# Attention results leave PSUM on two engines and are added on GpSimd; loads of keys, values and plain weights are tied to units of attention

## The chip, the cores and the metric

One core of one Trainium2 chip. The engines are named as in the profile: PE (TensorE), ACT (ScalarE), DVE (VectorE), POOL (GpSimd), and SP (SyncE), which only issues DMAs here. PEld is PE's loading of weights. The metric is the device time of one execution in microseconds; the median of three runs before the change is 2777.72 us (2775.32 to 2780.29).

## The reference

One layer of an encoder, 2048 tokens (a grid of 32 rows by 64) of 1024 features, in float32:

```python
h = rms_norm(x, norm_mix)
q_a, k_a, v_a, q_b, k_b, v_b, g_a, g_b = split(h @ w_in)
y_a = windowed_gqa(q_a, k_a, v_a, sink)          # 8 heads of 64, 2 heads of keys, |t - s| <= 128
y_b = neighborhood_attn(q_b, k_b, v_b, rpb)      # 8 heads of 64, 8 x 16 neighbours on the grid
merged = sigmoid(g_a) * (y_a @ w_proj_a) + sigmoid(g_b) * (y_b @ w_proj_b)
x = x + merged @ w_out
x = x + square(relu(rms_norm(x, norm_mlp) @ w_up)) @ w_down
return rms_norm(x, norm_final)
```

## The kernel before

Products are made of split operands: a float32 matrix is kept as a high part (what TensorE's fp32r format holds) and the low rest, and each product is three matmuls (`mm3`, L193 to L196). PE therefore has most of the work.

**Stages.** The input projections (to about 530 us of the span) turn tiles of `h` and of `w_in` into q, k, v and gates, and store them in HBM. Attention A follows (to about 820), attention B (to about 1138), then the merge with `w_proj_a`, `w_proj_b` and `w_out` (to about 1490), the up projection and the down projection.

**Attention A** has 32 units, `attn_a(g, i)`: two groups of keys by 16 blocks of 128 tokens, four heads in each unit. A unit's first half loads q (L683, three buffers), makes four scores (L690, L691), adds bias and takes the maximum on DVE (L692 to L696), takes the exponential on ACT (L699), and scales by the reciprocal sum on POOL (L703). Its second half turns the probabilities on PE (L709), splits them (ACT `ph` L712, DVE `pl` L713), and multiplies with v into the one bank `av` (L714, L715). **Attention B**, `attn_b(h, j, ...)`, has 32 units too: eight heads by four strips of columns. The lines of the same steps are L818 (q), L821 (v), L831 (scores), L836 to L839 (bias and maximum), L842 (exponential), L846 (scaling), L858 (turning), L863 and L864 (`phb`, `plb`), L869 (bank `av`).

**The eviction.** v stands in two halves, high and low, in the columns of one weight tile. So the bank `av` holds 128 rows, of which the lower 64 (from the high v) and the upper 64 (from the low v) have to be added. ACT copies rows 64 to 127 to SBUF (L718, L876), DVE adds rows 0 to 63 from the bank (L719, L877), and `put` notes the store to HBM; the next unit's second half issues it with `flush` from ACT's queue (L173). As `av` has one buffer, the next unit's first product into it waits for the addition.

**Keys and values.** In A, `load_kv(g, m)` (L670 to L675) loads one half of a group's keys (three DMAs: one of 512 KB, two of 256 KB) and values (512 KB). All four calls are written ahead of the units. In B each head's keys are loaded by `load_k` (L804 to L811), and a bias is made on POOL for three of the four strips (L799) from rows `braw` that SP loads into one buffer (L793).

**Fillers.** What is left of the input projections for the second half of the tokens, four tiles of v and sixteen of gates, is written as a generator of 40 pieces (`fill`). One piece is 24 matmuls into bank `mm`. A tile's weights come through `slice_of`: a load of 512 KB into `raw` (L184, three buffers), a cast on ACT and a subtraction on POOL (`split_weights`, L176, L177) into `whl` (two buffers). `paced` ties each piece behind a product of an earlier unit, `lag` units back, with `tc.issue_after`; that orders what stands on that product's engine, PE. 22 pieces go to A, 18 to B. The loads of a piece are on SP and are not tied.

**Order.** The program is planned ahead of the run: a planner with a model of each instruction's time walks through the program, takes what is ready, and prefers what stands earlier in the text. Each engine then runs its instructions in that order. SP's and ACT's queues also issue the DMAs in order, and a DMA that waits for a buffer, or for an earlier DMA with the same semaphore, holds what is behind it. `tc.issue_after(ins)` puts what its block issues on the engine of `ins` behind `ins`; it orders the issue and waits for nothing else. `drive` starts a unit's first half two units ahead of the second half of the one that PE finishes.

**Memory.** Pools are stacked from both ends of SBUF. Attention A's `ka1`, `va1`, `qa`, `sa` and so on stand on the left, `va0`, `ka0`, `biasa0` on the right, in space that the input projections used. In the merge, the gate of `w_proj_b`'s half is loaded into `z` of the pool `wp` (L1167, L1168), which the fillers use too.

Of the kernel before, what the change touches and what calls it, by code (L numbers as in the profile page):

```python
# [22 lines left out]
P = 128  # L23
KC = D // P
NB = 4
BT = 512
# [66 lines left out]
def encoder_layer(ctx, tc, x, norm_mix, w_in, b_gate, sink, rpb, w_pa, w_pb, w_out,  # L93
# [28 lines left out]
    def T(pl, shape, dt, tag, bufs):  # L122
        n_t[0] += 1
        pl = pl[tag] if isinstance(pl, dict) else pl
        return pl.tile(shape, dt, tag=tag, bufs=bufs, name=f"{tag}_{n_t[0]}")
# [49 lines left out]
    def split_weights(raw, hl):  # L175
        A.copy(hl[:, 0], raw)  # L176
        G.tensor_tensor(out=hl[:, 1], in0=raw, in1=hl[:, 0].bitcast(F32), op=ALU.subtract)  # L177

    def slice_of(parts):

        raw = T(wp, [P, KC, P], F32, "raw", 3)
        at = 0
        for ap, n in parts:
            SY.dma_start(raw[:, at : at + n, :], ap.rearrange("(k p) f -> p k f", p=P))  # L184
            at += n
        hl = T(wp, [P, 2, KC, P], F32R, "whl", 2)
        split_weights(raw, hl)
        return hl
# [438 lines left out]
    masks = pool("masks", side="right", stack=s_m)  # L627
    hpl = pool("hT", side="left", stack=s_h)
    s_a = ExitStack()
    ap_ = pools(s_a, "left", ("ka1", "va1", "qa", "sa", "ph", "pl", "ya", "sta", "biasa1"), "a")  # L630
    ap_.update(pools(s_a, "right", ("va0", "ka0", "biasa0"), "a"))
    b12 = tuple(T(hpl, PAGE, F32R, "hT", 2) for _ in range(2))
    for n, (h, l) in enumerate(zip(*map(halves, b12))):
# [7 lines left out]
    def v_tile(col):  # L641
        hl = slice_of([(cols(w_in[0], col), KC)])
        yield
        for b in (2, 3):
            ps = psum("mm", 2)
            feature_tile(ps, hl, hp[b])
            vt = T(wp, [P, BT], F32, "z", 3)
            A.copy(vt, ps)
            out = v_parts(col, b, vt, psum("mm", 2), T(wp, [P, 1024], F32, "v2", 1))
            for dst, t in out:  # L650
                SY.dma_start(dst, t)
            yield
# [4 lines left out]
    def make_bias_a(g):  # L657
        t = T(ap_, [P, 4, 384], F32, f"biasa{g}", 1)
        dist = t[:, 3]
        SY.dma_start(dist, dist_a)  # L660
        for h in range(4):
            G.tensor_scalar(t[:, h], dist, 2.0 ** -(4 * g + h + 1), 1.0, ALU.mult, ALU.mult)
        bias_a[g] = t

    done, began = [], []

    kas = [T(ap_, [P, 2, S], F32R, f"ka{g}", 1) for g in range(2)]
    vas = [T(ap_, [P, 16, P], F32R, f"va{g}", 1) for g in range(2)]
# [1 line left out]
    def load_kv(g, m):  # L670
        k, kd = kas[g][:, :, m * (S // 2) : (m + 1) * (S // 2)], ks_a[m][g]
        SY.dma_start(k[:, 0].bitcast(F32), kd)
        SY.dma_start(k[0:64, 1].bitcast(F32), kd[64:128])
        SY.dma_start(k[64:128, 1].bitcast(F32), kd[0:64])
        SY.dma_start(vas[g][:, 8 * m : 8 * m + 8].bitcast(F32), vs_a[m][g])  # L675

    def attn_a(g, i):
        c0, c1 = (1 if i == 0 else 0), (2 if i == 15 else 3)
        lo, hi = c0 * P, c1 * P
        n = hi - lo  # L680
        base = (i - 1) * P
        q = T(ap_, [P, 4, P], F32R, "qa", 3)
        began.append(SY.dma_start(q.bitcast(F32), qs_a[g][i // 8][:, i % 8]).ins)  # L683
        ka, v = kas[g], vas[g]
        s = T(ap_, [P, 4, 384], F32, "sa", 4)
        st = T(ap_, [P, 5, 4], F32, "sta", 6)
        mx, nm, sm, es, ri = (st[:, k, :] for k in range(5))
        for h in range(4):
            ps = psum("s", 3)
            PE.matmul(ps[:, :n], q[:, h, :], ka[:, 0, base + lo : base + hi], start=True, stop=False)  # L690
            PE.matmul(ps[:, :n], q[:, h, :], ka[:, 1, base + lo : base + hi], start=False, stop=True)  # L691
            V.tensor_tensor_reduce(out=s[:, h, lo:hi], in0=ps[:, :n], in1=bias_a[g][:, h, lo:hi], scale=1.0,  # L692
                                   scalar=sink_t[:, 4 * g + h : 4 * g + h + 1], op0=ALU.add, op1=ALU.max,
                                   accum_out=mx[:, h : h + 1])
        V.tensor_scalar(nm, mx, -1.0, None, ALU.mult)
        V.tensor_tensor(out=es, in0=sink_t[:, 4 * g : 4 * g + 4], in1=nm, op=ALU.add)  # L696
        A.activation(es, es, AF.Exp)
        for h in range(4):
            A.activation(s[:, h, lo:hi], s[:, h, lo:hi], AF.Exp, bias=nm[:, h : h + 1], accum_out=sm[:, h : h + 1])  # L699
        V.tensor_tensor(out=sm, in0=sm, in1=es, op=ALU.add)  # L700
        V.reciprocal(ri, sm)
        for h in range(4):
            G.tensor_scalar(s[:, h, lo:hi], s[:, h, lo:hi], ri[:, h : h + 1], 1.0, ALU.mult, ALU.mult)  # L703
        yield
        po = psum("av", 1)
        for c in range(c0, c1):
            pt = psum("pt", 2)
            for h in range(4):
                PE.transpose(pt[:, h * P : (h + 1) * P], s[:, h, c * P : (c + 1) * P], ident)  # L709
            ph = T(ap_, [P, 512], F32R, "ph", 3)  # L710
            pl = T(ap_, [P, 512], F32R, "pl", 3)
            A.copy(ph, pt)  # L712
            V.tensor_tensor(out=pl, in0=pt, in1=ph.bitcast(F32), op=ALU.subtract)  # L713
            PE.matmul(po, v[:, i - 1 + c, :], ph, start=c == c0, stop=False)  # L714
            last = PE.matmul(po, v[:, i - 1 + c, :], pl, start=False, stop=c == c1 - 1).ins  # L715
        done.append(last)
        t = T(ap_, [64, 512], F32, "ya", 2)
        A.copy(t, po[64:128, :])  # L718
        V.tensor_tensor(out=t, in0=po[0:64, :], in1=t, op=ALU.add)  # L719
        flush()  # L720
        put(y_a[g].rearrange("(h d) t -> d h t", d=64)[:, :, i * P : (i + 1) * P],
            t.rearrange("d (h q) -> d h q", h=4))
# [18 lines left out]
        while last and live:  # L741
            next(live.pop(0), None)

    def paced(filler, pieces, total, lag):

        for n in range(pieces):
            at = min(n * 32 // total - lag, 31)
            with tc.issue_after(done[at]) if at >= 0 else nullcontext():
                next(filler, None)

    def gate_tile(f, blocks):
        hl = slice_of([(cols(w_in[0], O_GA + f * P), KC)])
        yield
        for b in blocks:
            ps = psum("mm", 2)
            feature_tile(ps, hl, hp[b])
            z = T(wp, [P, BT], F32, "z", 3)
            A.copy(z, ps)
            A.dma_start(zg[b][0][f // 8, (f % 8) * P : (f % 8 + 1) * P, :], z)
            yield  # L760
# [1 line left out]

    fill = chain([v_tile(O_VB + t * P) for t in range(4)] + [gate_tile(f, (2, 3)) for f in range(16)])
    live = []
    for g in range(2):
        make_bias_a(g)
        for m in range(2):
            load_kv(g, m)
    drive((attn_a(g, i) for g in range(2) for i in range(16)), live, True)
    paced(fill, 22, 22, 3)  # L770
    del done[:]
    flush()
    s_a.close()
# [1 line left out]

    s_b = ExitStack()
    bp = pools(s_b, "right", ("braw", "biass", "biasl", "kb0", "qb", "kb1"), "b")
    bp.update(pools(s_b, "left", ("vb", "sb", "phb", "plb", "yb", "stb"), "b"))
    boff, bstart, btotal = bias_layout()
    masks = masks.tile([P, btotal], F32, tag="masks", bufs=1, name="masks_t")  # L780
    with tc.issue_after(began[20]):
# [31 lines left out]
    def attn_b(h, j, k, bias):  # L813
# [1 line left out]
        w, jt = B_W[j], JT[j]  # L815
        kp = 4 * w
        q = T(bp, [P, 4, P], F32R, "qb", 3)
        SY.dma_start(q.bitcast(F32), qs_b[t][e, :, j])  # L818
        yield
        v = T(bp, [P, 8, P], F32R, "vb", 3)  # L820
        SY.dma_start(v[: 4 * w].rearrange("p (b c) d -> p b (c d)", b=4).bitcast(F32),  # L821
# [49 lines left out]
                              skip_group_check=True).ins  # L871
                    first = False
        done.append(last)

        y = T(bp, [64, BT], F32, "yb", 2)
        A.copy(y, po[64:128, :])  # L876
        V.tensor_tensor(out=y, in0=po[0:64, :], in1=y, op=ALU.add)  # L877
        put(y_b[t].rearrange("(e d) (i j t) -> e d i j t", e=2, i=4, j=4)[e, :, :, j, :],
            y.rearrange("d (i t) -> d i t", i=4))

# [44 lines left out]

    first_y = load_y(0)
    first_load = last_dma[0]
    paced(fill, 18, 14, 4)
    s_h.close()


# [224 lines left out]
    for b in range(NB):  # L1156
# [3 lines left out]
        for f in range(8):  # L1160
            hl = slice_of([(cols(w_pa[0], f * P), 4), (cols(w_pb[0], f * P), 4)])
            parts = []
            for n in range(2):
                ps = psum("mm" if n == 0 else "s", 2 if n == 0 else 3)
                for c in range(4):
                    mm3(ps, hl[:, 0, 4 * n + c, :], hl[:, 1, 4 * n + c, :], yh[n][:, c], yl[n][:, c], c == 0, c == 3)
                g = T(wp, [P, BT], F32, "z", 3) if n else T(p4, [P, BT], F32, "z", 4)  # L1167
                SY.dma_start(g, zg[b][0][n, f * P : (f + 1) * P, :])  # L1168
                A.activation(g, g, AF.Sigmoid, bias=bg[:, 8 * n + f : 8 * n + f + 1])
                V.tensor_tensor(out=g, in0=ps, in1=g, op=ALU.mult)  # L1170
                parts.append(g)
            G.tensor_tensor(out=parts[0], in0=parts[0], in1=parts[1], op=ALU.add)
            A.copy(mh[:, f], parts[0])
            V.tensor_tensor(out=ml[:, f], in0=parts[0], in1=mh[:, f].bitcast(F32), op=ALU.subtract)
            if b == 0:
                with tc.issue_after(first_load):
                    load_wo(f)
# [243 lines left out]
```

## Time and profile before

| | us |
|---|---|
| median of three runs | 2777.72 |
| profiled execution, its own time | 2775.78 |
| its span, first to last instruction | 2773.9 |
| PE busy | 2657.5 (96%) |
| DVE busy | 1648.4 (59%) |
| ACT busy | 1274.8 (46%) |
| POOL busy | 836.1 (30%) |
| mean granted clock of PE | 0.983 |

A time in the span counts from its first instruction. In a window of the trace, "20.00, 13.64 (x61)" says that PE was busy 13.64 of 20 us with 61 instructions; the other engines follow, then the clock that the throttle granted to PE as a share of full speed, the share of time in which the DMA engines were busy, and what they moved. A line of the waits names the instruction that waited, what released it, the sum, how often, and the longest. A line of a timeline has the start, the duration, the engine and line, and the tiles (out<-in); what stands in brackets is the engine's idle time before it and what ended it. PEld, matmul ends and spans on POOL are modelled or rough.

### The profile page before, as it was taken

To read this page: it belongs to the slowest core of one execution; us is meant where nothing else is said; L and a number is where in the kernel's file an instruction comes from. 1 tells how busy PE (TensorE), PEld (TensorE's weight loads), DVE (VectorE), ACT (ScalarE), POOL (GpSimd) and SP (SyncE) were. 2 spreads that over 40 slices of the span, in tenths; PEclk is the share of its full clock that TensorE was granted. 3 is DMA by queue.
4 is the path that set the end of the run, shared out by engine and by line. 5 is a ranking of instruction groups with operands and counts; after the bars stand their busy time and mean duration, and the time that the engine had idled before them with its cause. 6 is when DMAs were issued, how large, how long until landed. Compare 5 with 4: busy or idle time off the path is not lost.

```text
span 2773.9 us, 35174 instructions
## 1 busy us (share of the span) xinstructions
PE 2657.5 (96%) x12248; PEld 2181.0 (79%) x12248; DVE 1648.4 (59%) x2443; ACT 1274.8 (46%) x2252; POOL 836.1 (30%) x669
## 2 busy tenths in 40 slices
PE   7999999899998888999999999989999999999998
PEld 6887778688877777778877788878888788888887
DVE  8655675476655656544335666686554644545666
ACT  6334343376654656534333544454444332332444
POOL 1111231143535554334231355565555000000000
PEclk9999999999998999999999999999999999999999
DMA  5756855845347774756444656564433954445555
GB/s 152 196 150 201 275 200 130 254 112 156 106 130 180 190 190 140 240 157 216 126 160 163 228 171 216 182 207 161 156 137 142 343 190 157 143 152 179 168 191 173
DMA packets 326130, 493.66 MB, mean 178 GB/s; under 512 B 28456, under 2 KB 149544, under 8 KB 323776
## 3 DMA queue, kind: packets, MB, share of 16 engines
q1 hardware_dynamic: 297024, 457.85, 52.6%
q10 hardware_dynamic: 28928, 33.56, 3.8%
q8 instruction: 97, 1.59, 0.2%
q14 instruction: 81, 0.66, 0.1%
HBM read 331.86 MB, written 159.45 MB: 177 GB/s over the span
## 4 chain that ended last, share of the span: by engine, by line
PE 80%; DVE 7%; DMA 6%; ACT 4%; issue 2%; POOL 1%; SPq 0%; ACTq 0%; DVEq 0%; POOLq 0%
PE b L240 14%; PE b L242 14%; PE b L241 14%; PE zb L240 5%; PE zb L242 5%; PE zb L241 5%; PE mm L194 3%; PE mm L195 3%; PE mm L196 3%; PE av L869 2%; PE pt L194 2%; PE pt L196 2%; PE pt L195 2%; PE pt L858 1%; DMA z<-zg 1%
## 5 line engine op out<-in xcount | busy, mean ns | idle before, releaser
L241 PE MATMUL b<-dwh,dah 128*128 128x512 f32 x896 | 348.5, 389 | 0.0
L242 PE MATMUL b<-dwh,dah 128*128 128x512 f32 x896 | 347.7, 389 | 0.0
L240 PE MATMUL b<-dwh,dah 128*128 128x512 f32 x896 | 338.1, 389 | 2.2 <-ACT dwh L236 2.2
L233 POOL TENSOR_TENSOR uc<-uc,uc 128x512 f32<-128x512 f32 x120 | 233.4, 1960 | 209.5 <-issue 135.9
L236 ACT CAST dah<-da 128x1024 fp32r<-128x1024 f32 (+1 forms) x128 | 121.0, 945 | 366.6 <-PE b L242 242.3
L240 PE MATMUL zb<-zh,zwhl 128*128 128x512 f32 x672 | 267.6, 401 | 8.7 <-DVE zc L233 3.8
L237 DVE TENSOR_TENSOR dah<-da,dah 128x1024 fp32r<-128x1024 f32 (+1 forms) x128 | 139.3, 1090 | 223.4 <-ACT dah L236 220.4
L241 PE MATMUL zb<-zh,zwhl 128*128 128x512 f32 x672 | 267.7, 399 | 1.8 <-DVE zh L237 1.8
L242 PE MATMUL zb<-zh,zwhl 128*128 128x512 f32 x672 | 264.3, 399 | 4.6 <-DVE zwhl L237 4.5
L240 PE MATMUL b<-ubh,uwhlb 128*128 128x512 f32 x592 | 230.8, 390 | 2.9 <-ACT mh L1207 1.6
L242 PE MATMUL b<-ubh,uwhlb 128*128 128x512 f32 x592 | 229.6, 389 | 2.6 <-DVE uwhlb L237 2.6
L241 PE MATMUL b<-ubh,uwhlb 128*128 128x512 f32 x592 | 230.4, 389 | 0.0
L233 DVE TENSOR_TENSOR uc<-b,uc 128x512 f32<-128x512 f32 x160 | 108.9, 688 | 189.1 <-PE b L242 152.2
L1311 POOL TENSOR_TENSOR st<-st,power 128x1 f32<-128x1 f32 x16 | 13.5, 857 | 614.3 <-DVE st L1310 614.2
L240 PEld LDWEIGHTS b<-dwh,dah 128*128 128x128 f32 x896 | 168.1, 188 | 37.4 <-ACT dwh L236 2.6
L241 PEld LDWEIGHTS b<-dwh,dah 128*128 128x128 f32 x896 | 168.2, 188 | 34.9
L242 PEld LDWEIGHTS b<-dwh,dah 128*128 128x128 f32 x896 | 168.2, 188 | 34.9
L177 POOL TENSOR_TENSOR whl<-raw,whl 128x1024 fp32r<-128x1024 f32 x52 | 129.1, 2483 | 117.1 <-ACT whl L176 117.1
L240 PEld LDWEIGHTS zb<-zh,zwhl 128*128 128x128 f32 x672 | 127.5, 190 | 42.2 <-issue 4.6
L242 PEld LDWEIGHTS zb<-zh,zwhl 128*128 128x128 f32 x672 | 127.6, 190 | 35.5 <-DVE zwhl L237 5.9
L241 PEld LDWEIGHTS zb<-zh,zwhl 128*128 128x128 f32 x672 | 128.0, 191 | 31.2 <-DVE zh L237 2.1
L237 POOL TENSOR_TENSOR zwhl<-zraw,zwhl 128x1024 fp32r<-128x1024 f32 (+1 forms) x24 | 57.5, 2401 | 255.6 <-ACT zwhl L236 254.0
(248 smaller groups left out, 6451.2 us busy)
## 6 DMA issues: line engine op xcount, KB each, us to landing
at<-uc SPq DMA_DIRECT2D x224, 256.0 KB
da<-at SPq DMA_DIRECT2D x96, 512.0 KB
dw<-in_w_down_dram SPq DMA_DIRECT2D x160, 256.0 KB
uraw<-in_w_up_dram SPq DMA_DIRECT2D x32, 1024.0 KB
zraw<-in_w_in_dram SPq DMA_DIRECT2D x22, 1024.0 KB
z<-zg SPq DMA_DIRECT2D x64, 256.0 KB
raw<-in_w_in_dram SPq DMA_DIRECT2D x20, 512.0 KB
xin<-in_x_dram SPq DMA_DIRECT2D x16, 512.0 KB
```

The lines of the kernel that those rows point to most:

```text
L177: G.tensor_tensor(out=hl[:, 1], in0=raw, in1=hl[:, 0].bitcast(F32), op=ALU.subtract)
L194: PE.matmul(ps, lh, rh, start=first, stop=False)
L195: PE.matmul(ps, lh, rl, start=False, stop=False)
L196: PE.matmul(ps, ll, rh, start=False, stop=last)
L233: return eng.tensor_tensor(out=out, in0=a, in1=b, op=op).ins
L236: A.copy(hi, src)
L237: eng.tensor_tensor(out=lo, in0=src, in1=hi.bitcast(F32), op=ALU.subtract)
L240: PE.matmul(ps, lh, rh, start=first, stop=False, skip_group_check=True)
L241: PE.matmul(ps, lh, rl, start=False, stop=False, skip_group_check=True)
L242: PE.matmul(ps, ll, rh, start=False, stop=last, skip_group_check=True)
L858: PE.transpose(pt[:kp, at + (i - i0) * P : at + (i - i0 + 1) * P], s[i][:, rr : rr + kp], ident)
L869: last = PE.matmul(po[:, i0 * P : (i0 + ni) * P], v[:kp, c, :], src[:kp, o : o + ni * P], start=first, stop=(c == 7 and z == 1), skip_grou ...
```

## The change

Three parts. (1) A new helper `both_parts` takes the place of the eviction in both attentions: ACT copies the upper half, DVE copies the lower half into a tile of its own (`ya0`, `yb0`, one buffer each), and POOL adds the two in SBUF. (2) In A only the first bias and the first `load_kv` are written ahead of the units. The other loads, and the second bias, are written before units 4, 8 and 12 and queued behind the q loads of units 2, 6 and 10. (3) The loads of `slice_of` are queued behind the q load of a unit that `paced` works out; in B the q loads are noted for it in `began_b`. And `z` in `wp` has two buffers in place of three.

```diff
+    load_after = [None]
+
     def slice_of(parts):
         raw = T(wp, [P, KC, P], F32, "raw", 3)
         at = 0
         for ap, n in parts:
-            SY.dma_start(raw[:, at : at + n, :], ap.rearrange("(k p) f -> p k f", p=P))
+            with tc.issue_after(load_after[0]) if load_after[0] else nullcontext():
+                SY.dma_start(raw[:, at : at + n, :], ap.rearrange("(k p) f -> p k f", p=P))
             at += n
...
+    def both_parts(pl, tag, po):
+
+        t, lower = T(pl, [64, 512], F32, tag, 2), T(pl, [64, 512], F32, tag + "0", 1)
+        A.copy(t, po[64:128, :])
+        V.tensor_copy(lower, po[0:64, :])
+        G.tensor_tensor(out=t, in0=t, in1=lower, op=ALU.add)
+        return t
...
-        t = T(ap_, [64, 512], F32, "ya", 2)
-        A.copy(t, po[64:128, :])
-        V.tensor_tensor(out=t, in0=po[0:64, :], in1=t, op=ALU.add)
+        t = both_parts(ap_, "ya", po)
         flush()
...
-    def paced(filler, pieces, total, lag):
+    def paced(filler, pieces, total, lag, loads):
         for n in range(pieces):
             at = min(n * 32 // total - lag, 31)
+
+            soon = (n + 2) * 32 // total - lag + 2
+            load_after[0] = loads[min(soon, 31)] if soon >= 0 else None
             with tc.issue_after(done[at]) if at >= 0 else nullcontext():
                 next(filler, None)
+        load_after[0] = None
...
-    for g in range(2):
-        make_bias_a(g)
-        for m in range(2):
-            load_kv(g, m)
-    drive((attn_a(g, i) for g in range(2) for i in range(16)), live, True)
-    paced(fill, 22, 22, 3)
+    make_bias_a(0)
+    load_kv(0, 0)
+
+    def all_a():
+        for g in range(2):
+            for i in range(16):
+                n = 16 * g + i
+                if n in (4, 8, 12):
+                    with tc.issue_after(began[n - 2]):
+                        if n == 8:
+                            make_bias_a(1)
+                        load_kv(*{4: (0, 1), 8: (1, 0), 12: (1, 1)}[n])
+                yield attn_a(g, i)
+
+    drive(all_a(), live, True)
+    paced(fill, 22, 22, 3, began)
...
-        SY.dma_start(q.bitcast(F32), qs_b[t][e, :, j])
+        began_b.append(SY.dma_start(q.bitcast(F32), qs_b[t][e, :, j]).ins)
...
-        y = T(bp, [64, BT], F32, "yb", 2)
-        A.copy(y, po[64:128, :])
-        V.tensor_tensor(out=y, in0=po[0:64, :], in1=y, op=ALU.add)
+        y = both_parts(bp, "yb", po)
...
-    paced(fill, 18, 14, 4)
+    paced(fill, 18, 14, 4, began_b)
...
-                g = T(wp, [P, BT], F32, "z", 3) if n else T(p4, [P, BT], F32, "z", 4)
+                g = T(wp, [P, BT], F32, "z", 2) if n else T(p4, [P, BT], F32, "z", 4)
```

The two other uses of `z` in `wp`, in `v_tile` and `gate_tile`, get two buffers in the same way, and the pools `ya0` and `yb0` join the lists of pools on the left.

More of the change, by code (lines that the diff above doesn't have):

```diff
@@ L629, in encoder_layer @@
     s_a = ExitStack()
-    ap_ = pools(s_a, "left", ("ka1", "va1", "qa", "sa", "ph", "pl", "ya", "sta", "biasa1"), "a")
+    ap_ = pools(s_a, "left", ("ka1", "va1", "qa", "sa", "ph", "pl", "ya", "ya0", "sta", "biasa1"), "a")
     ap_.update(pools(s_a, "right", ("va0", "ka0", "biasa0"), "a"))
@@ L646, in v_tile @@
             feature_tile(ps, hl, hp[b])
-            vt = T(wp, [P, BT], F32, "z", 3)
+            vt = T(wp, [P, BT], F32, "z", 2)
             A.copy(vt, ps)
@@ L663, in make_bias_a @@
         bias_a[g] = t
-    done, began = [], []
+    done, began, began_b = [], [], []
     kas = [T(ap_, [P, 2, S], F32R, f"ka{g}", 1) for g in range(2)]
@@ L756, in gate_tile @@
             feature_tile(ps, hl, hp[b])
-            z = T(wp, [P, BT], F32, "z", 3)
+            z = T(wp, [P, BT], F32, "z", 2)
             A.copy(z, ps)
@@ L777, in encoder_layer @@
     bp = pools(s_b, "right", ("braw", "biass", "biasl", "kb0", "qb", "kb1"), "b")
-    bp.update(pools(s_b, "left", ("vb", "sb", "phb", "plb", "yb", "stb"), "b"))
+    bp.update(pools(s_b, "left", ("vb", "sb", "phb", "plb", "yb", "yb0", "stb"), "b"))
     boff, bstart, btotal = bias_layout()
```

## The prediction

> **What bounds the kernel now.** I read the busy slices of the page first, then stretches of 20 us (windows), the waits of TensorE in the poor ones, and the timelines of the queues behind those waits. In the page's slices PE is the only engine near its limit:
>
> ```profile
> PE   7999999899998888999999999989999999999998
> ```
>
> So only time in which PE idles, or runs at a lower clock, can be won. Attention A runs from 537 to 820 us of the span, B from 820 to 1138. In the windows (span, busy time of PE, PEld, DVE, ACT, POOL, then granted clock, DMA share, GB/s):
>
> ```profile
> 540.00:560.00 20.00, 17.62 (x75) 14.87 (x76) 12.55 (x37) 8.75 (x25) 5.12 (x7) 0.80 0.74 227
> 600.00:620.00 20.00, 20.00 (x109) 17.05 (x108) 12.29 (x34) 11.74 (x28) 7.96 (x11) 1.00 0.39 110
> ...
> 820.00:840.00 20.00, 13.64 (x61) 10.08 (x61) 12.16 (x43) 10.88 (x32) 12.22 (x17) 0.78 0.93 256
> ...
> 860.00:880.00 20.00, 12.85 (x73) 11.27 (x72) 14.07 (x21) 9.19 (x22) 16.11 (x19) 0.80 0.66 175
> ```
>
> Between 560 and 820 PE idles 5.0 us in all (20.00 less busy, summed over 13 windows): that part of A has nothing to give. B idles 47 us, and its clock drops with the idling. The entry to A is the third place. PE's waits there (us, times, longest), and SP's timeline:
>
> ```profile
> PE s L690 <- DMA ks_b<-ze: 7.2, 1, 7.2
> PE s L691 <- DMA ka<-ks_a: 3.7, 1, 3.7
> ```
> ```profile
> 513.14 0.53 SPq L672 DMA_DIRECT2D ka<-ks_a  x1
> ...
> 521.77 0.39 SPq L675 DMA_DIRECT2D va<-vs_a  x1
> ...
> 532.21 0.38 SPq L672 DMA_DIRECT2D ka<-ks_a  x1
> ...
> 536.81 0.74 SPq L674 DMA_DIRECT2D ka<-ks_a  x1
> ```
>
> PE stops at 530.4 after its last filler and gets the first score of group 0 through at 542.4. The keys that end the wait come from the load of 536.81, which the chain of waits follows for 5.51 us to 542.32. The eight loads of 513 to 522 are 3 MB that nobody needs yet: group 1's, whose home is free sooner, and queue and lanes serve them first. In B (PE's own waits, 820 to 1140):
>
> ```profile
> PE av L869 <- DVE yb L877: 20.8, 15, 2.1
> PE pt L858 <- DVE plb L864: 9.8, 7, 5.5
> PE av L869 <- ACT phb L863: 9.0, 3, 4.5
> ```
>
> **The change, part by part.**
>
> *Eviction of the attention bank.* Now: ACT copies the upper half (0.58 us, L876), then DVE adds the lower (0.68, L877), then PE may write the one av bank. After: ACT's copy and a DVE copy side by side, so DVE's 0.68 and a hop of 0.06 leave the chain. One turn on the chain, then ACT's and DVE's timelines:
>
> ```profile
> 941.48 0.59 ACT yb L876
> 942.09 0.69 DVE yb L877
> 942.83 1.53 PE av L869 x9
> ```
> ```profile
> 942.08 1.07 ACT L863 CAST phb<-pt 96x512 fp32r<-96x512 f32 x2
> ```
> ```profile
> 942.70 1.28 DVE L864 TENSOR_TENSOR plb<-pt,phb 96x512 fp32r<-96x512 f32 x2
> ```
>
> PE could start at 942.12. But only the first pair's four matmuls (0.5 us) are then ready. The second pair wants its phb, which ACT casts after the copy (942.08 to 942.66), and the plb after that, at 943.38. That matmul ran at 943.52 before and can run at 943.44. So the turn wins 0.1 us, not 0.74: what is late next is ACT's own queue, exps, copy, cast. 15 such turns: 1.5 us. Bounds: 0 to 15 x 0.74 = 11. In A the same wait is 1.9 us over six turns (PE's waits on DVE ya); I take 1. The new DVE copy is not in the trace: DVE reads of 288 and 512 columns of a bank take 0.45 and 0.69 us (L836), so it costs DVE what the add did.
>
> *The add on GpSimd.* 64 adds on 64x512. The nearest row is L1172, 128x512, 1.30 us: 42 us of POOL in A and in B, where it is busy some 40% and 50%. Its reader is ACT's y store (flush), no longer DVE's next instruction. Two costs follow. First, DVE's small operations stop while POOL adds. DVE's timeline and then POOL's:
>
> ```profile
> 868.13 6.19 DVE L839 TENSOR_SCALAR stb<-stb 128x4 f32<-128x4 f32 x1
> ```
> ```profile
> 868.21 2.34 POOL L177 TENSOR_TENSOR whl<-raw,whl 128x1024 fp32r<-128x1024 f32 x1
> 870.51 3.77 POOL L799 TENSOR_TENSOR biasl<-braw,masks_t 128x384 f32<-128x384 f32 x3
> ```
>
> L839 has four columns, takes 0.16 us at best, and ended when POOL's additions did; PE then idled 5.54 us. The Trainium skill (GPSIMD Engine Reference, Specifications) says why: GpSimd's SBUF interfaces are shared with VectorE and contend with DVE's 2-port modes and with its two-input operations. The trace agrees (6.19 us), and the rule speaks against this change. How often would it strike? The add can start when POOL's four scalings (L846, 2.1 to 2.5 us from the reciprocal on) are done and then ends 3 to 4 us after the bank's copy. Laid into the trace, it ends 0.1 to 0.6 us before the next L839 in six turns of B (954.19 against 954.35), runs into it by 0.1 to 0.6 in three, and is far from it in most others. I take 1 us lost, bounds 0 and 13 (the third rival).
>
> Second, the store waits in ACT's queue for POOL, and casts stand behind it. I take 1 us, bounds 0 and 30 (second rival).
>
> *Loads of keys and v in A.* Eight of sixteen, then four, leave the entry. What remains there: bias, group 0's first 1.5 MB, three q, ks_b's stores. Group 0's home is free when the last zb matmul has read zwhl (524.7). At best the key loads go out at once, and the third lands 1.2 us of issue and 5.5 of transfer later: 531.5. At worst SP still puts four ks_b stores between the first and the second, as at 532.68 to 536, and nothing moves: 542.4. I take 533.5, a little over the best since the queue is emptier than the one that the 5.51 us was measured in, yet stores remain: 8.9 us, bounds 0 and 10.9. Clock: after the stop the filler's matmuls stood 0.43 apart, not 0.23, nine of them, 1.7 us; I leave that as a bonus that a shorter stop may not bring. The moved loads (12, 4.5 MB) now come beside units 2 to 12, where DMA is busy 0.39; q has three buffers, 24 us of lead, against some 7 us for 1.5 MB.
>
> *Loads of plain weights.* Each raw load goes behind a q load, about three units (24 us) ahead of its matmul, where it used to go three slices ahead, when a buffer came free. SP stood 57 us in A and 36 around B at L184 for that buffer; PE felt little of it, as the waits above show. At the entry 1.5 MB of five early slices go too (counted above). What is lost is lead: ACT's cast whl could now wait for its load (3.8 to 12.7 us from issue to landing in A) with casts of ph behind it. I take 1 us, bounds 0 and 8 (eleven slices by a cast's 0.7).
>
> *z from three buffers to two.* In the merge, ACT waits for z 44 times, 84 us, and PE hardly (10 us of waits in all from 1140 to 1560). A round trip of one buffer (load some 3, sigmoid 0.72, product 0.69, add 1.29) is about 6 us, two buffers serve an f every 3, and PE needs 5.6 per f. I take 0.5, bounds 0 and 4. In fillers, pieces are 12 to 20 us apart: nothing.
>
> Sum: -8.9 - 1.5 - 1 + 1 + 1 + 1 + 0.5 = -7.9 us. The profiled execution took 2775.78 (span 2773.9 and 1.9 around it), so 2767.9; it lies 1.9 under the median of 2777.72, and on that basis the forecast is **2769.8, say 2769**.
>
> **Rivals.**
>
> 1. *The bank was what held B.* If the new order also brings phb earlier, the 15 turns win 0.74 each (11 us). The clock then falls less: rows at 0.78 to 0.96 over B's 318 us are a loss of about 27 us (one less the clock, times the window, summed), of which I give a third, 9. With the entry's 9: 2777.7 - 29 = 2749. For: 20.8 is the largest wait in B. Against: the turn above. 0.14.
>
> 2. *The store blocks ACT (slower).* POOL works in order and waited for braw at L799 11 times, 52.8 us, up to 13.0. An add placed behind such a wait holds the y store, it holds ACT, and phb is late. The trace has one such stop, from another cause: the store of 1008.89 waited from 1003.4 (5.5 us), and PE lost 4.46. Laid behind POOL's bursts, the adds of 861, 893, 930 and 993 would end 9 to 17 us after the store's present place, 48 us together, of which PE would feel 0.8. With half of them so placed: 24 x 0.8 = 19 us, 3 more for the clock, less 9 for the entry: 2791. It decides from two of the four on; with one it is even. 0.19.
>
> 3. *The shared interface.* If every add of B meets an L839, it is late by up to 1.3 us. Delays of 2.19, 1.53 and 1.31 us cost PE 1.25, 0.65 and 0.38 in the trace: about 0.4 for 1.3, 32 times, 13 us; less 8, 2783. This is the rule cited above from the Trainium skill; three meetings in 32 speak against so much. 0.07.
>
> 4. *The entry stays.* SP's order is planned anew, and stores or a late first weight slice (the filler of 524.7 to 530 needs it) may take the place of group 1's keys. Then -0.0 to +2: 2778. 0.16.
>
> Forecast: 0.44.
>
> **How the numbers follow.** A measurement tells about 0.2% (5.6 us) from no change: faster is below 2772.2, slower above 2783.3. The forecast's own range is 2761 to 2774, nine tenths of it faster. Faster: 0.40 + 0.14 + 0.02 = 0.56. Slower: 0.19 + 0.03 (of rival 3) = 0.22. Same: 0.22. Range for eight in ten: 2747 to 2788; that leaves out about half of rival 1 and half of rival 2.
>
> **What would show it.** Right: the first A score before 535 and no half-clock row at 540; A's other windows at 19.5 or more; B's wait of av on the bank gone, but one on phb or plb in its place of nearly the same size. Wrong: an ACT store L173 that waits for POOL several us (rival 2), L839 with many durations over 1 us (3), PE waiting for ka beyond 540 (4), or B's windows above 19 at clock 1.00 (1). What I can't see is the planned order after the change: every number of B rests on ACT keeping exps, copy, cast.

## The result and the profile after

The changed kernel takes 2820.26 us in the median (2817.23 to 2829.38); the kernel before, run beside it, 2776.52. The ratio is 1.0163, 95% interval 1.0135 to 1.0191: 44 us slower, where 2769 was forecast. The profiled execution took 2822.0 us, with a span of 2820.2 (before 2773.9) and a mean clock of 0.975 (0.983).

The first question is in which stage the time went. From PE's timeline, in us of the span ("A" from the first score to the last product of attention A, "B" from there to the last product of attention B):

| | first score | A | B | rest | span |
|---|---|---|---|---|---|
| before | 537.7 | 282.3 | 316.4 | 1637.5 | 2773.9 |
| after | 538.6 | 288.6 | 362.1 | 1630.9 | 2820.2 |
| difference | +0.9 | +6.3 | +45.7 | -6.6 | +46.3 |

Nearly all of it is attention B. Two things make it up. PE idles 71.1 us in B, for 47.1 before. And the same 1546 matmuls keep it busy 291.0 us, for 269.3, at a mean granted clock of 0.854, for 0.914. The lower clock is enough for that: 269.3 x 0.914 / 0.854 is 288. So of the 45.7 us, 24 are idle time and 22 are matmuls that take longer. (The rest has the same 7087 matmuls, and PE idles 25.2 us in it, for 29.9; e16 comes back to this.) The page's busy slices of the changed kernel, and the granted clock under them, show the same place:

```profile
PE   7999999899998877899999999999999999999998
PEclk9999999999998888899999999999999999999999
```

The windows, with the columns of the prediction:

```profile
540.00:560.00 20.00, 19.66 (x93) 16.32 (x92) 8.89 (x33) 6.99 (x23) 1.84 (x4) 0.91 0.63 174
...
700.00:720.00 20.00, 16.80 (x85) 13.15 (x83) 15.30 (x25) 11.72 (x29) 18.53 (x21) 1.00 0.33 91
820.00:840.00 20.00, 14.79 (x62) 10.01 (x61) 12.41 (x37) 11.23 (x31) 9.49 (x12) 0.91 0.48 141
860.00:880.00 20.00, 14.14 (x64) 12.45 (x65) 8.73 (x22) 10.64 (x26) 13.12 (x14) 0.66 0.47 130
```

The row of 540 is better than it was (19.66 for 17.62): PE no longer stops a second time behind the first score, but that score is no earlier. At 860 the clock falls to 0.66. What PE, and then ACT, waited for in B (820 to 1190; us, times, longest):

```profile
PE av L892 <- DVE yb L684: 41.5, 17, 7.1
PE av L892 <- ACT phb L886: 17.7, 8, 7.1
```
```profile
ACT phb L886 <- POOL yb L685: 19.4, 3, 8.4
ACT whl L176 <- DMA raw<-in_w_in_dram: 17.5, 4, 7.3
...
ACT yb L683 <- POOL yb L685: 10.8, 1, 10.8
...
ACT z L771 <- POOL yb L685: 6.7, 1, 6.7
```

The wait of `av` on the bank did not go, it doubled (20.8 before), and ACT has two waits that it did not have in the kernel before: 36.9 us for POOL's addition (19.4 + 10.8 + 6.7), and 17.5 for `raw`. One stop in full, from the timeline of all engines:

```profile
859.87 2.96 POOL L822 TENSOR_TENSOR biass<-braw,masks_t 128x288 f32<-128x288 f32 x3 [7.57 <-DMA braw<-tab]
862.80 1.25 POOL L685 TENSOR_TENSOR yb<-yb,yb 64x512 f32<-64x512 f32 x1
...
864.08 0.55 ACTq L173 DMA_DIRECT2D y_b<-yb  x1
864.73 0.48 ACT L886 CAST phb<-pt 128x384 fp32r<-128x384 f32 x1 [8.44 <-POOL yb L685]
...
865.26 0.58 PE L892 MATMUL av<-phb,vb 128*128 128x256 f32 x1 [7.12 <-ACT phb L886]
```

Read it downwards: POOL waits 7.57 us for `braw`, makes the bias, and only then the addition that stands behind it. The store in ACT's queue waits for the addition, the cast behind the store idles 8.44 us, and PE 7.12. That is the mechanism of the prediction's second rival. The eviction itself, from another window of the same timeline:

```profile
920.02 0.58 ACT L683 COPY yb<-av 64x512 f32<-64x512 f32 x1
...
920.71 0.68 DVE L684 COPY yb<-av 64x512 f32<-64x512 f32 x1 [0.50 <-ACT yb L683]
```

The two copies are not side by side. DVE's begins 0.11 us after ACT's end, in the median of the 64 units 0.10, and what it waits for is ACT. The bank leaves after 1.37 us in the median, for 1.30 with the addition before: no sooner.

### The profile page after: what moved, and what is told of

It reads as the page before. It is cut to its first block, busy times and chain, and to the rows that moved or that the text cites. A ratio compares the mean times of both kernels' runs of the same rounds, so it can differ in the third digit from the quotient of the medians.

```text
span 2820.2 us, 35092 instructions
## 1 busy us (share of the span) xinstructions
PE 2677.6 (95%) x12248; PEld 2199.3 (78%) x12248; DVE 1644.7 (58%) x2443; ACT 1275.6 (45%) x2252; POOL 916.7 (33%) x733
## 4 chain that ended last, share of the span: by engine, by line
PE 67%; DMA 5%; DVE 3%; ACT 2%; POOL 2%; issue 1%; SPq 0%; ACTq 0%; POOLq 0%; DVEq 0%
PE b L243 14%; PE b L244 14%; PE b L245 14%; PE mm L197 3%; PE mm L198 3%; PE mm L199 3%; PE pt L197 2%; PE pt L198 2%; PE pt L199 2%; DMA braw<-tab 2%; PE av L892 2%; PE pt L720 1%; ACT sb L865 1%; PE pt L881 1%; PE s L197 1%
## 5 line engine op out<-in xcount | busy, mean ns | idle before, releaser
L243 PEld LDWEIGHTS b<-dwh,dah 128*128 128x128 f32 x896 | 168.1, 188 | 36.9 <-ACT dwh L239 2.0
L244 PEld LDWEIGHTS zb<-zh,zwhl 128*128 128x128 f32 x672 | 126.8, 189 | 31.7 <-DVE zh L240 3.1
```

The lines of the kernel that those rows point to most:

```text
L243: PE.matmul(ps, lh, rh, start=first, stop=False, skip_group_check=True)
L244: PE.matmul(ps, lh, rl, start=False, stop=False, skip_group_check=True)
```

## The experiments

The theories at the start. **Store**: the y store waits in ACT's queue for POOL's addition, and casts wait behind it. **Late**: ACT's cast of a tied weight slice waits for its load, and casts of `phb` wait behind it. Rivals: POOL's 42 us of additions in each attention are themselves too much; the two z buffers; the bank. Ratios are to the kernel before, run beside each kernel, with 95% intervals; they are not quotients of the medians.

### The parts one at a time

e1: the changed kernel with the old eviction.

```diff
-        t = both_parts(ap_, "ya", po)
+        t = T(ap_, [64, 512], F32, "ya", 2)
+        A.copy(t, po[64:128, :])
+        V.tensor_tensor(out=t, in0=po[0:64, :], in1=t, op=ALU.add)
```
and the same in B.

> The changed kernel with the old eviction (ACT copies the upper half, DVE adds the lower from the bank); the tied loads, the later keys and the two z buffers stay. Theory E (the eviction: the store waits in ACT's queue for POOL's addition): most of the loss goes, 2775 to 2785 us; what is left is the late raw load, up to 10 us. Theory L (the tied weight loads hold ACT's casts): the loss stays, 2805 to 2820. In the trace of the changed kernel ACT waited 42 us for POOL's additions and 17.5 us for raw in attention B; shared out by these, the loss of 44 us would be 31 of E and 13 of L, so about 2789.

Measured: 2803.58 us, ratio 1.0095 (1.0079 to 1.0111): below theory L's range, and 15 us above the shared figure.

e2: the kernel before with `both_parts` (the diff above the other way round) and two z buffers.

> The kernel before with the new eviction alone, and two z buffers in place of three, without which the new tiles have no room. Loads as before. Theory E: 2805 to 2820 us, with POOL's additions again ending the waits of ACT's phb casts in attention B. Theory L: 2775 to 2785. Shared out by ACT's waits: about 2808.

Measured: 2800.98 us, 1.0090 (1.0072 to 1.0109): below theory E's range.

e3: the kernel before with `load_after`, `began_b` and the new `paced`, and nothing else of the change.

> The kernel before with one part of the change alone, the weight loads of slice_of queued behind units' q loads. Theory E: within 8 us of before, 2777 to 2785, ACT's whl cast waiting a little for raw. Theory L: 2800 or more, with ACT's whl cast waiting 15 us or more for raw in attention B. Shared out by ACT's waits: about 2789.

Measured: 2808.26 us, 1.0107 (1.0087 to 1.0126).

e4: the kernel before with `all_a` in place of the four early calls of `load_kv`.

> The kernel before with one part alone, the keys and values of attention A after the first half group loaded behind the units 2, 6 and 10. By the prediction's step the first score comes 8.9 us earlier and the time is about 2768. By the rival that the entry stays, 2776 to 2779: the trace of the changed kernel has the first score at 538.6 (537.7 before), so I expect this one.

Measured: 2776.07 us, 0.9986 (0.9971 to 1.0001); first score at 540.1.

By stage (B against before): e1 +29.1, e2 +26.1, e3 +32.2 us. So there are two losses of nearly one size, 23 us (e2) and 30 (e3) alone, and 44 together. Sharing the loss out by ACT's waits (31 to 13) was wrong: the tied loads alone cost more than twice what that gave. The keys and values cost nothing and bring nothing that can be told; the first score comes no earlier. What e3's ACT waited for in B (820 to 1140), and one stop:

```profile
ACT whl L176 <- DMA raw<-in_w_in_dram: 43.0, 6, 11.0
```
```profile
898.49 0.43 SPq L187 DMA_DIRECT2D raw<-in_w_in_dram  x1
...
905.98 1.04 ACT L176 CAST whl<-raw 128x1024 fp32r<-128x1024 f32 x1 [11.05 <-DMA raw<-in_w_in_dram]
...
909.66 0.56 DVE L871 TENSOR_TENSOR plb<-pt,phb 128x384 fp32r<-128x384 f32 x1 [0.18 <-ACT phb L870]
...
910.37 0.45 PE L865 MATMUL pt<-ident,sb 128*128 128x128 f32 x1 [6.97 <-DVE plb L871]
```

ACT came to the cast at 894.9, before SP had even issued the load; the load took 7.5 us, the cast came 0.03 us after it landed, and the exponentials and the cast of `phb` stood behind it. Of the eight casts from 780 to 1130 us seven waited, 46.9 us in all. In the kernel before none did. For comparison, the load and the cast of the same slice in e5, where the tie is four units earlier:

```profile
844.55 0.43 SPq L187 DMA_DIRECT2D raw<-in_w_in_dram  x1
...
864.71 1.05 ACT L176 CAST whl<-raw 128x1024 fp32r<-128x1024 f32 x1
```

There the load takes 10.7 us, longer than in e3, but has landed 9 us before the cast, which waits for nothing.

### The price of the store, of POOL and of the buffers

e5 is told with the ties below. e6: e2 with all stores that `flush` issues on SP's queue, those behind attention B included.

```diff
     def flush(keep=0):
         while len(pending) > keep:
-            A.dma_start(*pending.pop(0))
+            SY.dma_start(*pending.pop(0))
```


> The kernel with the new eviction alone (e2_evict_only, 2801 us), but the y stores are issued from SP's queue in place of ACT's. Theory 'store' (the y store waits in ACT's queue for POOL's addition, and casts, exponentials and fillers' copies wait behind it): ACT no longer waits for POOL's yb, most of the 23 us goes, 2778 to 2787. Rival 'POOL' (the 42 us of additions on POOL delay the bias and the scaling, or stop DVE): stays at 2795 or more.

Measured: 2785.52 us, 1.0033 (1.0016 to 1.0050).

e7: e2 with the addition on DVE.

```diff
-        G.tensor_tensor(out=t, in0=t, in1=lower, op=ALU.add)
+        V.tensor_tensor(out=t, in0=t, in1=lower, op=ALU.add)
```


> The kernel with the new eviction alone (e2_evict_only, 2801 us), but DVE adds the two halves in SBUF in place of POOL. The bank still leaves by ACT's copy and then DVE's, the store stays in ACT's queue. Theory 'store' and rival 'POOL' both say that the loss goes: 2778 to 2790, a few us above before since DVE has 0.7 us more in each unit. If it stays at 2800, it is neither: then it is the copy by DVE, the order of the copies or the two z buffers.

Measured: 2781.28 us, 1.0019 (1.0003 to 1.0035).

e15: the kernel before with two z buffers and a spare addition.

```diff
         V.tensor_tensor(out=y, in0=po[0:64, :], in1=y, op=ALU.add)
+        spare = T(bp, [64, 512], F32, "yb0", 1)
+        G.tensor_tensor(out=spare, in0=y, in1=y, op=ALU.add)
```


> The kernel before with the old eviction, two z buffers, and behind each eviction a spare addition of the same size on POOL, whose result nobody reads. Theory 'store': POOL's additions themselves cost little, 2776 to 2785 us. Rival 'POOL' (its queue is late for scaling and bias, or it stops DVE's small operations): 2795 or more.

Measured: 2778.91 us, 1.0024 (1.0004 to 1.0045). There are 64 additions, in A too, as many as in the change. But they read one tile twice, and take 1.03 us each, where the change's take 1.28 (medians): 66 us of POOL for 82.

e16: the kernel before with `"z", 2` for `"z", 3` in all three places.

> The kernel before with two z buffers in place of three and nothing else. The prediction took 0.5 us for it, bounds 0 and 4: 2776 to 2780. If it is the 5 us that stay in e7_add_dve: 2781 to 2783.

Measured: 2767.43 us in the median, below both expectations, ratio 0.9990 (0.9974 to 1.0007): no difference that can be told. But the traces show one. Behind attention B, PE idles 25.0 to 27.5 us in all ten kernels with two z buffers, and 28.9 to 31.7 in all ten with three, and nearly all of the difference lies 350 to 900 us behind B's end. That accounts for most of the 6.6 us by which the rest of the changed kernel is shorter; why a smaller pool does this stays open.

ACT's waits for POOL's addition in B, in e2:

```profile
ACT sb L848 <- POOL yb L682: 11.5, 2, 5.9
ACT phb L869 <- POOL yb L682: 11.1, 2, 7.9
...
ACT z L764 <- POOL yb L682: 8.7, 2, 5.7
...
ACT yb L680 <- POOL yb L682: 6.2, 1, 6.2
```

That is 37.5 us in e2; in e6 and e7 ACT has no such wait, and B is 319.3 and 320.3 us long, for 342.5 in e2 and 316.4 before. So the store in ACT's queue is 22 to 23 us of B. With the additions on POOL and nobody waiting (e15) B is 317.4. e6, e7 and e15 land where theory "store" put them; rival "POOL" at its price (2795 or more) falls. At a smaller price it stays: e16 is e15 without the additions, and 11 us faster (2767.43 for 2778.91; in ratios, 0.9990 for 1.0024). So the additions cost something by themselves, though nobody waits for their results, 9 to 11 us, and about as much as e6 keeps (9 us). e7, which has no addition on POOL but one more operation on DVE, keeps 5. What stays lies in A more than in B: A is 289.1 us long in e6, 286.7 in e7 and 285.3 in e15, for 282.3 before.

### The bank, and both mended

e10: the changed kernel, the weight loads four units earlier.

```diff
-            soon = (n + 2) * 32 // total - lag + 2
+            soon = (n + 2) * 32 // total - lag - 2
```


> The changed kernel with one constant altered: the weight loads are tied four units earlier (as in e5_raw_early). If the parts add, the changed kernel's 2820 falls by the 44 us between e3 and e5, to 2776 to 2782; what stays above e5's 2764 is then the eviction, less than the 23 us it cost alone. If the two losses hid each other's waits (in sum they were 51 and together 44), 2783 to 2790. If the eviction's waits for POOL were themselves caused by late casts, 2770 or less.

Measured: 2800.36 us, 1.0088 (1.0061 to 1.0114): a miss, 10 us above the highest figure. The late loads took 20 us of the changed kernel, not 44.

e11: e10 with e6's edit.

> The changed kernel with the weight loads tied four units earlier and the y stores issued by SP in place of ACT. By theory 'store' the rest of the eviction's price goes but for the 9 us that e6_store_sp kept: 2768 to 2776. If it is no faster than e10_after_raw_early, the store in ACT's queue is not what the eviction costs here.

Measured: 2781.93 us, 1.0015 (0.9999 to 1.0031): 6 us above the expected range, and no longer clearly above the kernel before. The two mendings take 38 of the 44 us: 20 (2820.26 to 2800.36) and 18 (to 2781.93). B is 319.0 us, 2.6 above before.

e12: e10 with the copies in the other order.

```diff
-        A.copy(t, po[64:128, :])
         V.tensor_copy(lower, po[0:64, :])
+        A.copy(t, po[64:128, :])
```


> As e10_after_raw_early, but in the eviction DVE's copy of the lower half is written ahead of ACT's of the upper. In the trace of the changed kernel DVE's copy begins about 0.1 us after the end of ACT's every time. Theory 'one after the other' (the second reader of the bank is ordered behind the first): now ACT's copy begins 0.1 us after DVE's ends, the bank leaves no sooner, and the time is within 8 us of e10, rather above, since ACT's queue now stands for DVE's 0.68 us. If the two copies overlap in this order, the bank leaves 0.6 us sooner and PE's wait of av on the bank halves.

Measured: 2810.53 us, 1.0129 (1.0098 to 1.0160), 10 us above e10, 2 more than expected. In all 64 units ACT's copy now starts after the end of DVE's, at best 0.03 us and in the median 1.53 us behind it; PE waits for ACT's copy:

```profile
PE av L892 <- ACT yb L684: 11.4, 9, 3.5
```

In e10 the same wait of B was 18.5 us (on DVE's copy), so it fell by more than a third, which an overlap would have done too; but the copies overlap in no unit. So whichever copy is written first, the other waits for it: the program orders the two readers of the bank. That the chip would run them side by side is what the Trainium skill gives to expect ("PSUM — Partial Sum Buffer", section "PSUM bank collisions raise a hardware error"): two engines may use one bank at the same time in different groups of 32 partitions, and these are rows 0 to 63 and 64 to 127. No run here shows an overlap, because the order was made ahead of the run; what a true overlap would bring was not tried.

### The ties' lead

e5: e3 with the edit of e10. e13, e17, e18 and e14: the same with `+ 1`, nothing, `- 3` and `- 5` in place of `- 2`, that is one, two, five and seven units earlier than in e3. A unit of B is about 10 us.

> The kernel before with the tied weight loads alone (as e3_raw_only, 2808 us), but tied four units earlier. In e3_raw_only nearly every cast of raw in attention B started within 0.03 us of its load's landing; the loads took 6 to 11.5 us there and were issued at the last moment. Theory 'late' (the tie asks for the load a transfer's time too late, ACT waits in order, casts of phb behind it): no cast waits any more, 2775 to 2783 us. Rival 'tied at all' (the tie rearranges the planned order, or the loads collide with those of B): stays above 2795.

> As e3_raw_only, but the weight loads are tied one unit earlier (about 10 us in attention B). The casts of e3 waited up to 11 us, mostly 4 to 8, so by theory 'late' one unit takes nearly all of the waiting: 2766 to 2780 us and at most 10 us of ACT's casts waiting for raw in B. If the tie's place in the plan matters rather than the lead: anywhere up to 2808.

> As e3_raw_only, but the weight loads are tied two units earlier. In ACT's planned order the first three casts of attention B still stand 2 to 22 places later than in the kernel before, the last ones at its places or two behind. By the theory that the cast's place decides, the first three wait for their loads and the others little: 2785 to 2800 us. If only lead counts, 20 us of it hide every load: 2764 to 2783.

> As e3_raw_only, but the weight loads are tied five units earlier, one more than e5_raw_early (2764 us) and two fewer than e14_raw_seven (2783). The casts of attention B stand at the places of the kernel before. Theory: no cast waits for raw, and the time lies between the two, 2764 to 2783; where in it tells whether e5's gain is the tie's or one plan's.

> As e3_raw_only, but the weight loads are tied seven units earlier (three more than e5_raw_early, 2764 us). Theory 'late': nothing more to win, 2760 to 2770. If early loads get in the way of the entry, where e5 has its first score at 534, the first score is later and the time 2770 to 2778, as before.

| earlier by | kernel | us | ratio | B, us | casts from 780 us on that waited | their wait, us |
|---|---|---|---|---|---|---|
| 0 | e3 | 2808.26 | 1.0107 | 348.6 | 7 | 46.9 |
| 1 | e13 | 2809.99 | 1.0150 (1.0121 to 1.0179) | 349.4 | 7 | 51.1 |
| 2 | e17 | 2808.66 | 1.0120 (1.0095 to 1.0146) | 347.0 | 7 | 38.9 |
| 4 | e5 | 2763.82 | 0.9952 (0.9938 to 0.9966) | 306.2 | 0 | 0 |
| 5 | e18 | 2775.71 | 0.9994 (0.9978 to 1.0009) | 313.4 | 0 | 0 |
| 7 | e14 | 2783.25 | 1.0031 (1.0015 to 1.0048) | 324.2 | 0 | 0 |

e5 came out 11 us below its expected range, and e14 above both of its own, though its first score is early (535.9).

In the number of waits it is a step, not a slope, and the first form of theory "late" fell with it: 10 us of lead (e13) should have hidden a wait of 4 to 8 us, and hid nothing. The loads of e13 went out 14 to 21 us earlier (833.4 for 847.0, 879.8 for 898.5, 931.2 for 951.9), and ACT came to its casts earlier too (841.9 for 850.0, 888.1 for 894.9, 939.2 for 950.9). The casts had moved along in the planned order.

Counted in ACT's order of instructions, the casts of 859, 906 and 959 in e3 have the places 642, 685 and 742; they are 637, 684 and 736 in e13, 627, 664 and 728 in e17, 617, 662 and 717 in e5, and 605, 662 and 717 in e18, e14 and the kernel before. At these last places a cast comes right behind a filler (before: pieces end at 865 and 917, casts start at 865.9 and 917.4), when the filler has read the slice whose home in `whl` is wanted, and the load has long landed. (e5 has luck in it: its cast of 823.45 comes 0.1 us after its load lands, and that of 1039.28 0.4 us.) At the others the load comes last: in e3 the last product that read from a `whl` had ended at 849.3 and 949.1, 9 and 10 us before the casts of 859 and 959. I take it that the planner puts the cast where its model has the load land. The model's times are in no trace, so this is inferred from where the casts went. The loads of B took 5.1 to 17.7 us from issue to landing in e3, e13 and e17, a spread that no single figure of a plan can meet, and ACT stands for the difference.

e17 missed its own expectation: its later casts are at most two places behind those of before, and one of them still waited 12.2 us. Perhaps the load and the home come free at nearly one time by the plan, which would be no cover either. So the mended theory: a tie costs as soon as it makes the load the last condition of an instruction in a busy engine's order, and lead helps only when it changes that. It fits the six kernels, but only two were forecast by it, and one of those (e17) missed: that the late loads cost the time is shown, by which rule the plan makes them late is not.

Among the three without waits the time still spreads by 19 us, and rises with the tie's lead. I have no cause for that. Each kernel is planned anew: B takes 303.8 us in e4, 316.4 before and 324.2 in e14, and none of them has a wait of these two kinds. e5's 13 us under before are measured, but that they come from the tie is not shown, since e18 and e14 lack them.

### The entry to attention A

e8: e4 with the homes exchanged.

```diff
-    kas = [T(ap_, [P, 2, S], F32R, f"ka{g}", 1) for g in range(2)]
+    kas = [T(ap_, [P, 2, S], F32R, f"ka{1 - g}", 1) for g in range(2)]
```
and the same for `vas` and `biasa`.

> The kernel with the later loads of keys and values alone (e4_kv_only, 2776 us), but group 0 of attention A gets the homes of group 1 (on the left, free at 513 us in the trace of before) and group 1 those of group 0. Theory 'home' (the first keys waited for the last matmul of the input projections, 531.8, because their home was read by it): the first score comes at 530 to 534, not 540, and the time falls by 6 to 9 us, to 2767 to 2770, unless attention B then starts later, since its tiles on the right get group 1's place only at 820; then 2776 or more. Rival 'transfers' (the keys are late because of the queue): the first score stays at 538 or later.

Measured: 2781.13 us, 1.0020 (1.0002 to 1.0037); the first score comes at 527.1. SP and PE in e8:

```profile
513.00 0.53 SPq L672 DMA_DIRECT2D ka<-ks_a  x1
...
527.09 0.28 PE L690 MATMUL s<-ka,qa 128*128 128x256 f32 x1
```

In the changed kernel the same load goes out at 531.67 and PE stands for it:

```profile
538.64 0.98 PE L701 MATMUL s<-ka,qa 128*128 128x256 f32 x3 [8.70 <-DMA ka<-ks_a]
```

Theory "home" holds: with a free place the load stands ahead of the stores of `ks_b`, and the score comes even before the expected 530. In the changed kernel the queue has a share too: PE's last filler matmul there ends at 529.95, and SP issues the keys 1.7 us later, behind two stores of `ks_b` that waited for their data until 530.32. The 13 us won at the first score (540.1 in e4) are given back: B takes 321.9 us for e4's 303.8, with a granted clock of 0.71 from 820 to 860 (0.91 in e4); a later B the expectation allowed. SP's first load of `braw` goes out at 811.8, behind A's last product, for 696.6 in e4, and POOL waits for `braw` 16.1 us between 785 and 850, for 3.1 in e4.

e9: both parts that move loads, the weights as in e5, without the eviction and the two z buffers.

> Both parts of the change that move loads, without the new eviction and with three z buffers: keys and values later as in e4_kv_only, weight loads tied four units earlier as in e5_raw_early (2764 us). If the two add, 2762 (e4 was 1.8 below before). The entry to attention A should be no better than in e5, since group 0's keys still wait for their home: first score at 534 to 540. If the 4.5 MB of keys beside the units get in the way of the earlier weights, 2768 or more.

Measured: 2773.14 us, 0.9991 (0.9974 to 1.0008): not the sum. First score at 542.5, later than expected and 8.5 us later than in e5; B as in e5 (306.9 for 306.2). e5 stays the fastest of all, below both kernels.

## Why the prediction was wrong

It said faster with 0.56, and 2769 us in a range from 2747 to 2788; measured were 2820. By its own steps:

**What bounds the kernel** was right: time was lost where PE idled in B, and the clock fell with it. But the clock was priced too low. The second rival gave it 3 us; in B of the changed kernel the slower matmuls are 22 of 46 us, and in e2, which has that rival's mechanism without the tied loads, 10 of 26 (PE busy 279.6 us for 269.3).

**Loads of plain weights is the step that failed most.** "I take 1 us, bounds 0 and 8 (eleven slices by a cast's 0.7)". Alone it cost 30 us (e3), out of the changed kernel 20 (2820 to e10's 2800). The step named the right wait and priced it by the cast. A cast that comes too early costs what is left of its load, up to 12.6 us (e13), and with it everything behind it in ACT's order. It also took for lead the distance of the load from its matmul, "24 us". The distance that counts is from the load to the cast. The row that told of this was used: issue to landing 3.8 to 12.7 us, a spread of 9 us, and eight casts from late A on, which bounds the waiting at 72 us; it was 46.9 in e3.

**The add on GpSimd, second cost**: "I take 1 us, bounds 0 and 30". Measured 15 (e2 to e6) and 18 (e10 to e11). The mechanism was the second rival's. Its 19 us of stops and 3 for the clock come to 22, as does B's loss from the store (22 to 23), but the shares were others: from e6 to e2 PE idles 15 us more in B, and its matmuls take 8 us more. The forecast's 1 us was the error: no working stands behind it, while the four adds laid into POOL's bursts (48 us) stood in the text.

**The add on GpSimd, first cost** (rival 3, DVE's small operations): "I take 1 us, bounds 0 and 13". The operations with four columns that took over 0.5 us, each less 0.2, sum to 23.4 us in A and B before and to 24.1 after, as if nothing had changed. That pair misleads: the sum is 15.2 in e1, which is the changed kernel without the additions, and 41.6 in e15 for 23.8 in e16. Over all kernels it is 24.1 to 43.4 us in the seven with additions on POOL, and 10.9 to 27.6 in the thirteen without. What part of that PE feels is not shown; e15 is 11 us slower than e16. One stop is of the rival's kind, at 714 in A, in the window of 16.80 above:

```profile
714.14 5.33 DVE L711 TENSOR_TENSOR sta<-sta 128x4 f32<-128x4 f32 x1
715.23 3.00 POOL L822 TENSOR_TENSOR biass<-braw,masks_t 128x288 f32<-128x288 f32 x3
718.20 1.25 POOL L685 TENSOR_TENSOR ya<-ya,ya 64x512 f32<-64x512 f32 x1
```

It ends as POOL's addition does. The rule of the Trainium skill (GPSIMD Engine Reference, Specifications) is seen again.

**Eviction of the bank**: -1.5 and -1 us were taken, and the premise was wrong: the copies are ordered, not side by side, so DVE's 0.68 never left the chain. That the change does not do what it says should have been a rival here. With the new eviction alone (e2) PE's wait on the bank in B is 18.0 us, for 20.8 before, and in e10 18.5: the 41.5 of the changed kernel came with the late casts. What true side-by-side copies would bring, no run shows.

**Loads of keys and v**: -8.9 us were taken; the first score is 0.9 later, and PE idles 8.7 us at the entry, for 10.9 in two stops before. Rival 4 (0.16) had it. The failed sentence is "Group 0's home is free when the last zb matmul has read zwhl (524.7)". In the kernel before the load of the bias beside the keys waits until the fillers' last matmul (530.45), and the first of group 0's keys goes out behind it, at 532.21; in e4 the two go out at 532.15 and 533.00, right behind the end of that matmul at 532.18. e8 shows what a free home gives.

**z from three buffers to two**: 0.5 us of cost was taken; e16 shows no cost that can be told, and PE's idle time behind B is some 4 us shorter.

**The sum.** The errors do not cancel: entry 10, weights 20 to 30, store 15 to 18. Of the 44 us, e10 and e11 account for 38. What is left in e11 can't be told from nothing in the time; by its trace the first score is 4.0 us later than before, A 3.8 and B 2.6 us longer, and the rest 5.9 shorter. The additions' own price would fit into it, but that is not shown for e11.

## What to carry to other kernels

When a load is tied to a place, ask what the instruction that reads it would otherwise have waited for. If the load becomes its last condition, an engine that runs in order will stand for every microsecond by which the plan was optimistic, and the bound to write down is the spread of the loads' times by their number, not the instruction's own length. Price the clock with the stop: here it cost PE nearly as much again. A result that is finished on an engine with waits of its own should not be stored from the queue of an engine that others wait for: the same additions cost 23 us with their stores on ACT and 9 on SP. And a kernel to which one thing is added needs a control with everything else alike: against the kernel before the spare additions cost 4 us, against e16 11.

## What the runs showed that I had not expected

A load of 512 KB of weights took 3.8 us from issue to landing in a quiet stretch and up to 18.0 us in B (e14, issued at 955.9), where DMA was busy 0.79 of the time (940 to 980). An addition of two tiles of 64x512 takes POOL 1.28 us, hardly less than the 1.29 of one with twice the rows (L1172 before). And ACT, busy 52% of B in the changed kernel, sets its pace all the same when one instruction in its order stands.
